# A gated layer with two attentions: six Strassen groups in the input projection, tanh gates, the bias summed behind FFN 1, and attention's filler at two rates

## The chip, the cores and the metric

One core of a Trainium2 chip runs the whole layer. The metric is the device time of one execution in microseconds (us), the median over runs. The engines are TensorE (PE; its weight loads are PEld), VectorE (DVE), ScalarE (ACT), GpSimd (POOL) and SyncE (SP). DMAs are issued on SP's and GpSimd's queues. "L94" is line 94 of the kernel before.

## The reference

The input x has 1024 tokens of 1024 features, all float32. One layer is computed:

```python
h = h + 0.5 * swiglu(rms_norm(h, ffn1_norm), ffn1_w_gate, ffn1_w_up, ffn1_w_down)      # 1024 -> 2816 -> 1024
z = rms_norm(h, mix_norm) @ w_in             # 1024 -> 4352: qa ka va (512 each) qb (512) kb vb (128 each) ga gb (1024 each)
ya = neighbourhood_attention_2d(qa, ka, va, na_rpb)        # 8 heads of 64, a window of 8 x 16 on a 16 x 64 grid, learned bias
yb = windowed_gqa_sink(rope(qb), rope(kb), vb, sink)       # 8 heads on 2 key heads, |i-j| <= 128, a sink logit per head
merged = sigmoid(ga) * (ya @ w_branch_a) + sigmoid(gb) * (yb @ w_branch_b)
h = h + merged @ w_out
h = h + 0.5 * swiglu(rms_norm(h, ffn2_norm), ffn2_w_gate, ffn2_w_up, ffn2_w_down)
return rms_norm(h, final_norm)
```

## The kernel before

**Precision.** Every float32 operand is split into a high half (a copy that rounds to the matmul's input type, on ScalarE, L93) and a low half (the rest, a subtraction on VectorE, or GpSimd where it is given as `eng`, L94). A product is three matmuls, high x high, high x low, low x high (`mm3`, L141 to L150: L145, L147, L149). A matmul has a 128x128 weight tile and streams 512 columns.

**Strassen.** The large products (FFN gate and up, FFN down, part of the input projection, W_out) use seven products of half-size blocks instead of eight (Strassen-Winograd). `products` (L233) runs groups of two pairs of 128-column chunks; for one group it does P1, P2, P5, P6, P7, P3, P4 for two members m, and calls `after` (here `store_z`, L879) with the PSUM banks, which adds the products up, on ScalarE or VectorE (L911, L913), and stores the finished halves in DRAM. `at_end(n)` is called with the number n of weight tiles left, down to 0; `hook` ties work to such an n.

**Order of the stages.** FFN 1's gate and up by hand-written order and then by `products` (to about 432 us); FFN 1's down product, class `Down` (L507); `transition` (L161: normalise and turn the rows, while the down product's tail is done a row block at a time); the input projection's groups (`pg`, to about 842 us); the attention (842 to 1127 us); branch A and the merge with the gates; W_out's product, again `Down`; a second transition; FFN 2 the same way.

**Down.** It has 7 products (P2, P1, P5, P6, P3, P7, P4) x 11 entries. An entry is 12 matmuls. `prep` (L560 to L563, then two splits) prepares an entry's two operands a ring of entries ahead: for P5, P6, P3 the weight blocks are first subtracted, on VectorE and, for half of P6 and all of P3, on GpSimd (L563, L565). `loads[e]` are functions that are called when entry e is reached.

**Projection hooks.** The rotary embedding reads z back from DRAM, does three VectorE operations and stores zr_d (`rope`, all at one n). `v_b` loads v, `order_v` reorders its columns by a ScalarE copy, `turn_v` transposes it. `q_b`, `k_b` load zr_d and split queries and keys. `keep_u` reloads a part of the projection's input and splits it into the place of an operand of the last group, for the gate chunks that are computed later.

**Attention.** 64 units: 32 of B (8 query blocks x 4 head pairs) and 32 of A (4 head pairs x 8 query blocks). A unit goes through `scores` (L1278, L1279, then on VectorE the sum with bias or mask and the row minimum of the negated scores, L1283, on ScalarE the exponential, L1286, and the normalisation), one step later `turn` (L1299) and two steps later `values` (L1313 for A, L1318 for B), whose `write` copies half of the output to SBUF on ScalarE (L1252, L1231) and adds it on VectorE (L1253, L1256, L1233). The bias of A's heads, already laid out in DRAM, is summed with the mask by `load_bias` (L1073) for each head pair.

**Filler.** Between these matmuls TensorE gets `filler` steps of 6 matmuls: the gate chunks that `products` did not do (14 x 8 steps), branch B (8 output chunks x 4 steps, with a weight split, a sigmoid on a gate row block and a multiplication for each), and two chunks of branch A (6 steps). `filling` spends (14*8 + 38 - 44)/64 = 1.656 steps per unit, the rest follows behind the last unit. Then branch A's other chunks run (`a_order`), each with `a_prep` (load of a gate, sigmoid, L1393), a multiplication and a sum, and `combine` builds W_out's Strassen operands.

A scheduler orders each engine's instructions from this program; `keep_in_program_order` (`pin`) keeps an instruction at its place in the program.

## Time and profile before

| | |
|---|---|
| median of 3 runs | 1934.88 us (1934.86 to 1935.12) |
| span of the profiled execution | 1934.8 us |
| VectorE busy 1000 to 1050 us (attention) | 45.66 of 50 us |
| VectorE busy 456 to 534 us (FFN 1 down) | 77.51 of 78 us |
| granted TensorE clock in those stretches | 1.00 |

The page gives each engine's busy time and the chain of work that ended last, followed back from the last instruction. "Idle before, releaser" in a group's row is how long the engine stood idle ahead of these instructions, and what ended it. In a stretch's row, busy time and the number of instructions stand for PE, PEld, DVE, ACT and POOL, then the granted clock, the share of the DMA engines and GB/s. A timeline's rows are start, duration, engine, line, output <- inputs, and in brackets the idle time before with what ended it. Matmuls overlap, so a single matmul's duration is longer than what it adds to the time.

### The profile page before, as it was taken

The numbers are of one execution on the slowest core, as the hardware profiler recorded it, in microseconds if no ns is written. First come the engines' busy times: TensorE is split into PE (matmuls) and PEld (weight loads), VectorE is DVE, ScalarE is ACT, GpSimd is POOL, SyncE is SP. The second block draws the span as 40 slices with busy tenths as digits, with TensorE's granted clock in tenths as the row PEclk, the third lists the DMA queues.
The fourth block names the chain that finished last, engine by engine and source line by source line (L and its number), as shares of the span: only waits on it lengthen the run. The fifth ranks groups of instructions, "written<-read, shape, count | busy, mean of one in ns | idle before, by whom it ended". The sixth has DMA issues, their size and how long they took to land.

```text
span 1934.8 us, 25499 instructions
## 1 busy us (share of the span) xinstructions
PE 1922.2 (99%) x8956; PEld 1603.1 (83%) x8956; DVE 1437.1 (74%) x2560; ACT 943.6 (49%) x1827; POOL 295.5 (15%) x432
## 2 busy tenths in 40 slices
PE   9999999999999999999999999999999999999998
PEld 7888888888888888888888888878888888888886
DVE  7987765668957788678888857889676566569864
ACT  6532333344446543477877862365333333344453
POOL 0011110013300112211122231010111001005210
PEclk9999999999999999999999999999999999999999
DMA  6344323286234478553458576533423323493341
GB/s 261 100 167 163 129 104 128 86 289 225 88 109 137 159 223 250 185 163 104 116 134 195 184 242 210 169 140 133 147 87 109 126 87 109 140 355 104 112 144 61
DMA packets 151745, 298.70 MB, mean 154 GB/s; under 512 B 14912, under 2 KB 64448, under 8 KB 151616
## 3 DMA queue, kind: packets, MB, share of 16 engines
q1 hardware_dynamic: 123072, 210.53, 33.6%
q0 software_dynamic: 27824, 85.48, 13.3%
q8 instruction: 71, 1.16, 0.3%
q10 hardware_dynamic: 720, 1.05, 0.1%
q14 instruction: 58, 0.48, 0.1%
HBM read 210.50 MB, written 88.27 MB: 154 GB/s over the span
## 4 chain that ended last, share of the span: by engine, by line
PE 88%; issue 7%; POOL 1%; DMA 1%; DVE 1%; ACT 1%; POOLq 0%; SPq 0%; ACTq 0%; DVEq 0%
PE g L149 16%; PE g L147 16%; PE g L145 16%; PE d L149 11%; PE d L147 11%; PE d L145 11%; PE d L1299 2%; PE g L1313 1%; PE g L1318 1%; PE d L1278 1%; PE d L1279 1%; POOL zs_d L889 1%; PE d L138 1%; POOL z_d L891 1%; DMA zr_d<-xs 0%
## 5 line engine op out<-in xcount | busy, mean ns | idle before, releaser
L145 PE MATMUL g<-ar,ws 128*128 128x512 f32 x1128 | 423.1, 395 | 0.6 <-ACT fa L911 0.6
L147 PE MATMUL g<-ar,ws 128*128 128x512 f32 x1128 | 417.2, 390 | 0.9 <-DVE ar L94 0.5
L149 PE MATMUL g<-ar,ws 128*128 128x512 f32 x1128 | 416.1, 390 | 0.2 <-DVE ws L311 0.2
L145 PE MATMUL d<-ar,ws 128*128 128x512 f32 x736 | 282.4, 391 | 0.3 <-ACT ar L810 0.2
L147 PE MATMUL d<-ar,ws 128*128 128x512 f32 x736 | 281.9, 390 | 0.3 <-DVE ar L812 0.3
L149 PE MATMUL d<-ar,ws 128*128 128x512 f32 x736 | 281.6, 390 | 0.5 <-DVE ws L311 0.5
L147 PEld LDWEIGHTS g<-ar,ws 128*128 128x128 f32 x1128 | 211.8, 188 | 46.2 <-DVE ar L94 1.0
L149 PEld LDWEIGHTS g<-ar,ws 128*128 128x128 f32 x1128 | 211.7, 188 | 45.5 <-DVE ws L311 0.7
L145 PEld LDWEIGHTS g<-ar,ws 128*128 128x128 f32 x1128 | 206.4, 188 | 37.8 <-ACT fa L911 1.0
L311 DVE TENSOR_TENSOR ws<-raw,ws 128x512 fp32r<-128x512 f32 x204 | 139.6, 690 | 99.6 <-ACT ws L308 98.8
L308 ACT CAST ws<-raw 128x512 fp32r<-128x512 f32 x204 | 125.1, 620 | 140.6 <-PE g L149 64.4
L145 PEld LDWEIGHTS d<-ar,ws 128*128 128x128 f32 x736 | 138.3, 188 | 29.7 <-ACT ar L810 0.6
L147 PEld LDWEIGHTS d<-ar,ws 128*128 128x128 f32 x736 | 138.4, 188 | 29.6 <-DVE ar L812 0.6
L149 PEld LDWEIGHTS d<-ar,ws 128*128 128x128 f32 x736 | 138.4, 188 | 29.4 <-DVE ws L311 0.7
L93 ACT CAST ws<-raw 128x512 fp32r<-128x512 f32 (+1 forms) x121 | 81.0, 669 | 144.0 <-PE d L149 61.8
L94 DVE TENSOR_TENSOR ws<-raw,ws 128x512 fp32r<-128x512 f32 (+1 forms) x119 | 93.7, 789 | 59.8 <-ACT ws L93 59.3
L414 POOL DMA_DIRECT2D hid<-fx x91 | 49.3, 542 | 431.5 <-DVE fx L474 304.9
L93 ACT CAST ar<-raw 128x512 fp32r<-128x512 f32 (+1 forms) x83 | 56.0, 679 | 94.8 <-PE g L147 55.0
L94 DVE TENSOR_TENSOR ws<-ar,ws 128x512 fp32r<-128x512 f32 x114 | 98.3, 867 | 3.8 <-ACT ws L93 3.7
L145 PE MATMUL g<-ws,ws 128*128 128x512 f32 x232 | 91.0, 392 | 0.0
L149 PE MATMUL g<-ws,ws 128*128 128x512 f32 x232 | 90.5, 390 | 0.0
L147 PE MATMUL g<-ws,ws 128*128 128x512 f32 x232 | 90.3, 389 | 0.0
(313 smaller groups left out, 3607.4 us busy)
## 6 DMA issues: line engine op xcount, KB each, us to landing
raw<-hid SPq DMA_DIRECT2D x70, 512.0 KB
hid<-fx POOLq DMA_DIRECT2D x91, 256.0 KB, 2.4
ar<-in_ffn_w_down_dram SPq DMA_DIRECT2D x32, 512.0 KB
raw<-in_ffn_w_up_dram SPq DMA_DIRECT2D x31, 512.0 KB
raw<-in_ffn_w_gate_dram SPq DMA_DIRECT2D x27, 512.0 KB
raw<-in_w_in_dram SPq DMA_DIRECT2D x27, 512.0 KB
hid<-fa POOLq DMA_DIRECT2D x51, 256.0 KB, 2.7
ar<-zs_d POOLq DMA_DIRECT2D x48, 256.0 KB, 5.3
```

The lines of the kernel that those rows point to most:

```text
L93: nc.scalar.copy(dst_hi, src)
L94: (eng or nc.vector).tensor_tensor(dst_lo, src, f32v(dst_hi), op=ALU.subtract)
L138: nc.tensor.transpose(pt[:, c * P:(c + 1) * P], xs[:, (half * 4 + c) * P:(half * 4 + c + 1) * P], ident)
L145: nc.tensor.matmul(b, lhs[0], r[0], start=first, stop=False, **kw)
L147: nc.tensor.matmul(b, lhs[0], r[1], start=False, stop=False, **kw)
L149: nc.tensor.matmul(b, lhs[1], r[0], start=False, stop=last, **kw)
L308: nc.scalar.copy(w[0][:, :512], a)
L311: nc.vector.tensor_tensor(w[0][:, 512:], a, f32v(w[0][:, :512]), op=ALU.subtract)
L414: nc.gpsimd.dma_start(hid[PRODUCTS.index(p), i], src)
L889: nc.gpsimd.dma_start(d[ch * P:(ch + 1) * P, cols], t)
L891: nc.gpsimd.dma_start(z_d[ch * P:(ch + 1) * P, cols], c)
L1299: nc.tensor.transpose(pt[:, i * P:(i + 1) * P], un["pr"][s][:, i * P:(i + 1) * P], ident)
```

## The change

- `groups` gets a sixth entry, gate chunks 20 to 23, which leave the filler's list (10 chunks of 8 steps stay). In the last group P4 is done ahead of P3 (`last`).
- FFN 1's down product gets, at entries 8+5h and 11+5h for head h = 0..7, the fetch of a laid-out bias and two VectorE adds with the mask, stored to DRAM (bm_d) on GpSimd's queue. The attention then loads finished sums (`fetch_bias`); `load_bias` goes.
- The gates use tanh(x/2) where a sigmoid stood; the multiplication adds 1 to it in the same instruction, and the factor 2 is taken back by W_out's scale, 1.0 to 0.5.
- Rotation: loads at one n, the three VectorE operations at n-4, n-5, n-6, one head block every 6. `order_v` goes; chunk 17's eviction writes the new order.
- `write` of B units: one VectorE add of 64x256 in place of two of 64x128; the sink column is copied once for two heads.
- Filler: 80 gate steps over units 0 to 49 (1.6 a unit), 28/14 = 2 a unit from 50 on, nothing spent ahead. Branch B fetches its weights and gates a chunk earlier; its splits' high halves and openings are pinned; splits of outputs move from GpSimd to VectorE.
- The last A output's split into slots 22 and 23 is done in two halves in `write`.
- The second transition (`ahead=3`) does one more block of W_out's tail ahead of a turn.

```diff
-    def split(dst_hi, dst_lo, src, eng=None):
-        nc.scalar.copy(dst_hi, src)
+    def split(dst_hi, dst_lo, src, eng=None, late=False):
+        hi = nc.scalar.copy(dst_hi, src)
+        if late:
+            pin(hi)
...
+    def bias_add(h):
+        for e in range(2):
+            o = biased[0][4 + e]
+            pin(nc.vector.tensor_tensor(o.rearrange("p (d r w) -> p d r w", d=3, r=ROWS),
...
+            nc.gpsimd.dma_start(bm_d[h, e], o)
+
+    for h in range(8):
+        down.loads.setdefault(8 + 5 * h, []).append(lambda d, h=h: bias_fetch(h))
+        down.loads.setdefault(11 + 5 * h, []).append(lambda d, h=h: bias_add(h))
...
+    groups = [[(12, 13), (14, 15)], [(16, 17), (0, 1)], [(4, 5), (8, 9)], [(2, 3), (6, 7)], [(10, 11), (18, 19)],
+              [(20, 21), (22, 23)]]
...
-    for c in range(4):
-        hook(14 * (NG - 1) - 8 - 3 * c, rope, c)
-    hook(14 * (NG - 2) - 6, rope, 4)
-    hook(14 * (NG - 2) - 12, v_b)
-    hook(14 * (NG - 2) - 14, order_v)
-    hook(14 * (NG - 3) - 12, turn_v)
+    for c in range(5):
+        n = 14 * (NG - 1) - 8 - 6 * c
+        hook(n, rope_load, c)
+        for step in range(3):
+            hook(n - 4 - step, rope, step, c)
+    hook(14 * (NG - 3) - 10, v_b)
+    hook(14 * (NG - 4) - 2, turn_v)
...
-    hook(0, keep_u)
+    hook(1, keep_u)
...
+    held = [main.tile([P, 512], F32, tag="hs", bufs=6, name=nm_("hs")) for _ in range(6)]
...
+    def fetch_bias(hp):
+        for s in range(2):
+            for e in range(2):
+                nc.sync.dma_start(bias_at(hp, s, e), bm_d[2 * hp + s, e])
...
-        split(t[:, :512], t[:, 512:], r, eng)
+        split(t[:, :512], t[:, 512:], r, eng, True)
...
+    def open_gate(dc):
+        r = mix["rb", dc]
+        pin(nc.scalar.activation(r, r, AF.Tanh, scale=0.5))
...
-    rate = (nfill - 44) / 64.0
-    spent = 3.0
+    n_b = 50
+    rates = (len(gates) * 8 / n_b, 28 / (64.0 - n_b))
+    spent = 0.0
...
-            split_y(Y_A[n - 60], 512 + (n - 60) * P, nc.gpsimd)
+            split_y(Y_A[n - 60], 512 + (n - 60) * P, nc.vector)
...
-    split(slot(22), slot(23), fa[:, 3072:4096])
...
-    down = Down(4, wo[0], 1.0, place, quarter, {k: left_d[i] for i, k in enumerate(("P5", "P6", "P3", "P7"))},
+    down = Down(4, wo[0], 0.5, place, quarter, {k: left_d[i] for i, k in enumerate(("P5", "P6", "P3", "P7"))},
...
-        nc.scalar.activation(r, r, AF.Sigmoid)
+        nc.scalar.activation(r, r, AF.Tanh, scale=0.5)
...
-    merge.into(transition(down2, gain, to_strassen, behind(hg), 2), hg)
+    merge.into(transition(down2, gain, to_strassen, behind(hg), 2, 3), hg)
```

## The prediction

> **What bounds the kernel now.** I read the page first: engine shares, then the chain that ended last.

> ```profile
> span 1934.8 us, 25499 instructions
> PE 1922.2 (99%) x8956; PEld 1603.1 (83%) x8956; DVE 1437.1 (74%) x2560; ACT 943.6 (49%) x1827; POOL 295.5 (15%) x432
> PE 88%; issue 7%; POOL 1%; DMA 1%; DVE 1%; ACT 1%; POOLq 0%; SPq 0%; ACTq 0%; DVEq 0%
> ```

> TensorE is the bound nearly everywhere. So an edit counts in two ways only: by the matmuls it adds or removes, and by the moments at which TensorE must wait. The profiled execution spans 1934.8 us and the median of the runs is 1934.88 us, so the sum is made against 1934.9 us. The mean of one matmul (about 390 ns in the page's groups) is no price, because matmuls overlap. The price is read from busy time by stretch: columns are PE, PEld, DVE, ACT, POOL busy (instructions), granted clock, DMA share, GB/s.

> ```profile
> 100.00:150.00 50.00, 50.00 (x222) 41.42 (x221) 43.88 (x72) 17.31 (x30) 7.96 (x15) 1.00 0.50 171
> 456.00:492.00 36.00, 36.00 (x160) 29.80 (x160) 35.72 (x36) 14.86 (x26) 20.58 (x13) 1.00 0.31 105
> 492.00:522.00 30.00, 30.00 (x134) 24.83 (x133) 29.79 (x34) 12.82 (x23) 14.74 (x9) 1.00 0.24 80
> 522.00:534.00 12.00, 12.00 (x54) 9.95 (x53) 12.00 (x21) 5.47 (x10) 0.00 (x0) 1.00 0.51 149
> 534.00:552.00 18.00, 18.00 (x81) 14.89 (x80) 9.92 (x17) 6.96 (x14) 0.00 (x0) 1.00 0.37 110
> 1000.00:1050.00 50.00, 50.00 (x304) 44.23 (x303) 45.66 (x146) 40.70 (x107) 12.02 (x23) 1.00 0.70 175
> 1128.00:1178.00 50.00, 50.00 (x221) 41.17 (x220) 16.73 (x28) 23.71 (x30) 10.29 (x8) 1.00 0.77 258
> ```

> In the first row 222 matmuls of 128x512 take 50.00 us with TensorE never idle: 50/222 = 0.2252 us each, at a granted clock of 1.00. The next rows matter as much: from 456 to 534 us, inside the down product of FFN 1, VectorE is busy 77.5 of 78 us. Work added to VectorE there has no idle time to fall into.

> **The change part by part.**

> *Sixth Strassen group.* Four gate chunks leave the attention's filler, where each costs 8 steps of 6 matmuls (192 in all), and become a group of 7 products x 2 chunks x 4 weight blocks x 3 matmuls = 168. That is 24 fewer, and the built order of the changed kernel has 24 fewer 128x512 matmuls and the same number of every other TensorE form. **-24 x 0.2252 = -5.4 us.** The group's evictions are of the kind that the five groups before already hide.

> *Bias and mask behind FFN 1.* Sixteen VectorE adds leave the attention for FFN 1's down product; in the built order eight of them stand ahead of the operand splits for its entry 33, the first of P6. Where TensorE stands close behind VectorE is read from the two timelines (start, duration):

> ```profile
> 519.07 1.78 DVE L94 TENSOR_TENSOR ar<-ar,ar 128x512 fp32r<-128x512 f32 x1
> 521.38 0.68 DVE L94 TENSOR_TENSOR ar<-ar,ar 128x512 fp32r<-128x512 f32 x1
> 521.98 0.68 DVE L94 TENSOR_TENSOR ws<-raw,ws 128x512 fp32r<-128x512 f32 x1
> 522.01 0.39 PE L147 MATMUL g<-ar 128*128 128x512 f32 x1
> L1073 DVE TENSOR_TENSOR fa<-raw,masks 128x384 f32<-128x384 f32 x16 | 8.5, 550 | 0.1
> ```

> The split that ended at 519.07+1.78 = 520.85 feeds the matmul at 522.01: a lead of 1.16 us, the smallest of this stage. Neighbouring starts (521.38, 521.98) lie 0.60 apart for a 0.68 operation, so in a queue an operation costs some 0.08 less than its duration: 0.47 for the 0.55 add. Eight cost 8 x 0.47 = 3.8 us; less the lead, TensorE waits **+2.7 us** there. The lower end is 0, if part of the collisions with GpSimd (1.78 against 0.68 us) fall elsewhere; the upper 5, if the adds meet GpSimd too (two of eight slowed by 1.1 us). The other eight adds fall where VectorE is busy 9.92 of 18 us: free. Their stores go on GpSimd's queue, which has 36.00-20.58 us to spare, and their loads on SP's.

> *Attention.* VectorE and ScalarE per unit, before:

> ```profile
> L1233 DVE TENSOR_TENSOR xs<-g,s 64x128 f32<-64x128 f32 x64 | 18.0, 281 | 1.0 <-ACT s L1231 0.2
> L1253 DVE TENSOR_TENSOR s<-g,s 64x256 f32<-64x256 f32 x32 | 13.2, 411 | 2.6 <-ACT s L1252 2.3
> L1282 DVE COPY fa<-nsk 128x1 f32<-128x1 f32 x60 | 7.9, 142 | 0.5 <-ACT fa L1286 0.5
> L94 POOL TENSOR_TENSOR ar<-raw,ar 128x1024 fp32r<-128x1024 f32 x6 | 14.8, 2464 | 22.0 <-ACT ar L93 22.0
> L94 DVE TENSOR_TENSOR ar<-raw,ar 128x1024 fp32r<-128x1024 f32 x3 | 3.7, 1219 | 0.0
> ```

> VectorE loses two 64x128 adds for one 64x256 (18.0 us becomes 32 x 0.411 = 13.2), half the sink copies (4), and the 8.5 us above; it gains six 128x1024 splits that GpSimd did (6 x 1.22 = 7.3). But the filler is spent at 2 steps a unit in the last 14 units instead of 1.66, all of it branch B with its weight splits, openings and merges. Adding durations less 0.08 over the built order, VectorE needs in the four groups of four units at the end 1.03, 0.96, 0.91 and 0.99 of TensorE's time; the same sum for before gives at most 1.11 in one group, and in its heaviest stretch (45.66 and 40.70 busy of 50) TensorE lost little. I take **+1**, between 0 and +4 (14 units late by the 0.3 that one 64x128 add is).

> *Into the attention.* Two stalls of before stand here (the idle time in brackets), and ahead of them three links of the chain that leads to the first:

> ```profile
> 777.64 7.13 DMA zr_d<-xs
> 784.91 0.88 issue
> 785.79 0.60 ACT fa L911
> ```

> ```profile
> 786.43 0.50 PE L145 MATMUL g<-ar,ws 128*128 128x512 f32 x1 [0.56 <-ACT fa L911]
> 849.95 0.50 PE L147 MATMUL g<-ar,ws 128*128 128x512 f32 x1 [0.53 <-DVE ar L94]
> ```

> The first comes from ScalarE's reordering copy (order_v) that waits for a buffer until a rotation's store lands; the eviction L911 is stuck behind it. The copy is gone and the rotation's loads wait on SP: starts 785.49 to 786.43, less one matmul of 0.23, **-0.7 us**. The second is the late split of keep_u. Its hook moves one step earlier, but k_b's loads now stand on SP behind two fetches of bm_d, which wait for the buffer of the last product's evictions, that is for a store like this one (median us to landing last), and the keys had little to spare:

> ```profile
> g_d<-fa POOLq DMA_DIRECT2D x4, 256.0 KB, 4.2
> ```

> ```profile
> 839.84 1.23 DVE L94 TENSOR_TENSOR ar<-raw,ar 128x1024 fp32r<-128x1024 f32 x1 [0.74 <-ACT ar L93]
> 842.04 0.28 PE L1279 MATMUL d<-ar,ar 128*128 128x256 f32 x1
> ```

> The last key's split ended at 841.07 and the first matmul on a low half of a key began at 842.04: 0.97 us. I take a net **+0.5**, between -0.7 (the second stall goes too) and +2.4 (keys late by 4.2, less 0.97 and less the 0.8 by which P4 ahead of P3 frees that buffer sooner, about four matmuls).

> *The end of the attention.* Before, branch B and A's first chunks are left over behind the last unit's values: 36 steps x 6 matmuls and more, 228 x 0.2252 = 51 us. ScalarE's and VectorE's work for that unit's output lies under it:

> ```profile
> 1129.38 1.05 ACT L93 CAST ar<-fa 128x1024 fp32r<-128x1024 f32 x1
> 1130.45 1.28 ACT L1179 ACT_TABLE_LOAD   x1
> 1128.30 0.72 PE L147 MATMUL d<-ar,ws 128*128 128x512 f32 x2
> L1252 ACT COPY s<-g 64x256 f32<-64x256 f32 x32 | 11.9, 371 | 3.9 <-PE g L1313 3.1
> L1393 ACT ACTIVATE raw<-raw 128x1024 f32<-128x1024 f32 x8 | 8.5, 1061 | 7.7 <-DMA raw<-g_d 7.7
> L93 ACT CAST ws<-raw 128x512 fp32r<-128x512 f32 x10 | 6.2, 618 | 4.5 <-DMA raw<-in_w_branch_b_dram 4.0 <-PE d L149 0.2 <-DMA raw<-in_w_branch_a_dram 0.2
> L94 POOL TENSOR_TENSOR ws<-raw,ws 128x512 fp32r<-128x512 f32 x2 | 2.5, 1292 | 14.6 <-ACT ws L93 14.6
> ```

> After, the filler is spent (80 + 32 of 118 steps) when the last values end, and TensorE's next instruction is branch A's first matmul. Its weight is split only now: in the built order ScalarE does the copy of the last output (0.37), the tanh of a gate (1.06), the high half of output slot 22 (0.62 for 128x512) and only then the high half of that weight (0.62), which is pinned in program order. That is 2.67 us with TensorE idle. The low half follows on GpSimd (1.29); TensorE has four matmuls (0.9) before it needs it: 0.4 more. With 0.1 to 0.2 for each of five handovers, **+4 us**, between +3 (2.67+0.4, no handovers) and +5.5 (the tanh's load, which stands on SP behind six weight loads, comes 1.5 late). What is late next, the last output's split, has 36 matmuls = 8.1 us of cover.

> The tanh matters just here. The table load of before, 1.28 us at 1130.45, was hidden under the leftover; with a sigmoid it would now lie in this idle stretch. The built order has three table loads where before had four, none at this place. [...]

> *The merge's second transition.* One more block of W_out's product stands ahead of its fourth turn. Stalls of before here:

> ```profile
> 1290.35 1.06 PE L138 MATMUL d<-ident,xs 128*128 128x128 f32 x8 [0.80 <-DVE xs L129]
> 1295.59 0.50 PE L149 MATMUL g<-ar,ws 128*128 128x512 f32 x1 [0.24 <-DVE ws L311]
> 1315.96 0.50 PE L149 MATMUL d<-ar,ws 128*128 128x512 f32 x1 [0.48 <-DVE ws L311]
> ```

> The first stands ahead of the edit and stays. The order gives the later turns 12 to 18 whole matmuls between them, where before had blocks cut up: the other two may go. **-1**, between -2 and +1 (a stall like the first, in a new place).

> **Sum:** -5.4 + 2.7 + 1 - 0.7 + 0.5 + 4 - 1 = +1.1, so 1934.9 + 1.1 = **1936.0 us**: the saved matmuls are given back as waits.

> **The rivals.**

> *The gain arrives.* The adds in FFN 1 cost less than the lead (0 of 2.7), the last weight's split finds ScalarE free, say because the scheduler's order lets the tanh go late (3 of 4), the attention loses nothing (0 of 1): -5.4 + 0 + 0 - 0.7 + 0.5 + 3 - 1 = -3.6, and with the second transition at -2 and the entry at -0.7 it is -5.8: 1929 to 1931, say 1930. For it: VectorE has less work inside the attention. Against it: 35.72 of 36.00 busy, and the pinned order. Chance 0.27.

> *Slower: ScalarE and VectorE fall behind in the last 14 units.* The filler there is the work that needs them most, in order pinned with the units' own. If TensorE waits at each unit for one add, 14 x 0.28 = 3.9, and the chain at the end starts late with its 5.5: -5.4 + 2.7 + 3.9 - 0.7 + 0.5 + 5.5 - 1 = +5.5: 1940.4. It decides from the point where VectorE's need passes TensorE's time over a whole group (1.03 in the first of the four groups; 0.99 in the last). For it: those shares. Against it: the 1.11 group of before cost little. Chance 0.30, with the case that the bias adds meet GpSimd.

> *The change doesn't do what it says:* if tanh took a table of its own, eight openings among exponentials would cost 16 x 1.28 = 20 us of ScalarE. The order's three loads speak against it: below 0.01.

> **How the numbers follow.** A measurement tells about 0.2% from no change, 3.9 us: 1931.0 to 1938.8. The forecast (1933 to 1938.8 by itself) has 0.43, the gain's arrival 0.27, the slower case 0.30. The parts' ends summed whole give 1934.9 - 5.4 + (0+0-0.7-0.7+3-2) = 1929.1 and 1934.9 - 5.4 + (5+4-0.7+2.4+5.5+1) = 1946.7; that all meet at the upper end is improbable, so the range is 1928.5 to 1943.0. Faster 0.26, same 0.43, slower 0.31.

> **What would show it.** The matmul count falls by 24. In FFN 1's down product, idle time of TensorE behind L94 at the first of P6, near 522 us: 2.7 us. No stall at L911. Behind the last values, an idle stretch of 3 to 5.5 us ended by the pinned ScalarE copy, then a short one by GpSimd. If VectorE's eight adds open no gap at 522, or the last stretch is under 1 us, I am wrong and the time is near 1930; if gaps of some tenths stand at each of the last 14 units, it is near 1940.

## The result, and the profile after

| | before | after |
|---|---|---|
| median of the runs, us | 1935.12 (1934.86 to 1939.04, 5 runs) | 1944.10 (1942.62 to 1944.63, 5 runs) |
| span of the profiled execution, us | 1934.8 | 1942.3 |

The ratio is 1.0044, 95% interval 1.0033 to 1.0055: **slower by 0.44%**, some 8.5 us. The forecast was 1936.0, with a range of 1928.5 to 1943.0. The page of the changed kernel (its line 95 is the high half of a split, 98 the low half, 149 to 153 the three matmuls):

```profile
span 1942.3 us, 25526 instructions
PE 1919.9 (99%) x8932; PEld 1601.7 (82%) x8932; DVE 1450.5 (75%) x2527; ACT 944.5 (49%) x1836; POOL 293.5 (15%) x446
PE 85%; issue 6%; DVE 4%; ACT 2%; DMA 2%; POOL 1%; POOLq 0%; SPq 0%; DVEq 0%; ACTq 0%
L149 PE MATMUL g<-ar,ws 128*128 128x512 f32 x1096 | 416.4, 396 | 5.2 <-ACT ws L95 4.8
L149 PE MATMUL d<-ar,ws 128*128 128x512 f32 x760 | 293.2, 392 | 4.5 <-ACT ws L95 4.0
```

TensorE has 24 matmuls fewer (8956 to 8932) and its share of the chain falls from 88% to 85%. The new idle time stands ahead of matmuls that wait for the high half of a weight from ScalarE: 4.8 + 4.0 us in two groups, where before's page has no group of matmuls with more than this one:

```profile
L147 PE MATMUL g<-ar,ws 128*128 128x512 f32 x1128 | 417.2, 390 | 0.9 <-DVE ar L94 0.5
```

Where the time went is seen by stage. For each stage, "lost" is the time from its first matmul to the next stage's first, less the count of matmuls by shape times a price each (0.2252 us for 128x512, 0.171 for 128x384, 0.1165 for 128x256, 0.105 for 128x128). The wait behind the last values counts with the row that follows them. The prices lie a little under the median start-to-start times of before (0.227, 0.175, 0.119, 0.109), so some us of each long stage are no waits; the differences are what counts. The 24 saved matmuls do not appear in them, and kernels with unlike amounts of filler in a stage can be compared. The first 30 us stand alone: they lost 5.0 to 5.3 us in some executions and 6.3 to 7.1 in others, of kernels that share that code. In before's execution the clock was granted at 0.50 from 16 to 19 us, in that of after at 1.00, so this row is no effect of the change.

| lost, us | before | after | difference |
|---|---|---|---|
| first 30 us | 6.3 | 5.1 | -1.2 |
| rest of FFN 1 | 3.7 | 5.0 | +1.4 |
| transition and projection | 4.1 | 4.3 | +0.2 |
| first scores to last values | 10.1 | 18.9 | +8.8 |
| last values to second transition | 1.3 | 7.7 | +6.4 |
| second transition and FFN 2 | 8.1 | 5.3 | -2.8 |

With -5.4 for the matmuls the differences sum to +7.4, about that of the spans (7.5). Two rows hold the loss. Of the +8.8 in the first of them, 6.6 lie between 1081 and 1121 us, around branch B's first matmul (7.9 lost there, 1.3 in the like units of before), and 1.2 in the first 20 us; the 50 units ahead of branch B lose otherwise what they lost before. The idle stretches in them, from TensorE's timeline of the changed kernel (start, duration, and in brackets the idle time and what ended it):

```profile
888.74 0.41 PE L1358 MATMUL d<-ident,fa 128*128 128x128 f32 x2 [1.82 <-DVE fa L1349]
1094.83 0.72 PE L149 MATMUL d<-ar,ws 128*128 128x512 f32 x2 [3.98 <-ACT ws L95]
1106.92 0.50 PE L149 MATMUL g<-ar,ws 128*128 128x512 f32 x1 [0.79 <-ACT ws L95]
1164.70 0.50 PE L149 MATMUL g<-ar,ws 128*128 128x512 f32 x1 [0.80 <-ACT ws L95]
1175.32 1.22 PE L149 MATMUL g<-ar,ws 128*128 128x512 f32 x2 [3.20 <-ACT ws L95]
```

1094.83 is branch B's first matmul, 1175.32 branch A's. Both waited for their weight's split, and both were followed by something that the idle time alone doesn't show. These rows are stretches (PE, PEld, DVE, ACT, POOL busy with instructions, then the granted clock):

```profile
1094.00:1096.00 2.00, 1.17 (x5) 1.00 (x6) 1.92 (x4) 2.00 (x5) 0.54 (x1) 0.98 1.17 256
1096.00:1099.00 3.00, 3.00 (x12) 2.52 (x11) 1.85 (x5) 1.91 (x5) 0.00 (x0) 0.50 1.04 335
1099.00:1102.00 3.00, 3.00 (x14) 2.53 (x14) 2.42 (x6) 1.23 (x4) 0.00 (x0) 0.95 1.03 423
...
1172.00:1175.00 3.00, 0.12 (x2) 0.00 (x0) 1.95 (x6) 2.96 (x5) 0.00 (x0) 0.90 1.02 324
1175.00:1181.00 6.00, 5.68 (x13) 4.46 (x14) 0.47 (x1) 1.83 (x4) 4.99 (x4) 0.50 1.05 396
1181.00:1184.00 3.00, 3.00 (x14) 2.45 (x13) 0.00 (x0) 0.00 (x0) 0.00 (x0) 0.96 1.06 396
```

After the idle stretch the clock was granted at 0.50 for 3 us, then for 6. In the second of these stretches a matmul of 128x512 starts 0.427 us behind the one before it, against 0.227 at full clock (13 in the row of 6 us, which at 0.227 us each would take 3.0), so the two cost nearly half their length: about 1.5 and 3 us on top of the waits.

ScalarE at branch B's start, around the first of them, has no idle time left (no bracket in any row):

```profile
1090.93 0.61 ACT L1345 ACTIVATE fa<-fa,nmx 128x384 f32<-128x384 f32 x1
1091.45 0.19 ACT L1345 ACTIVATION_READ_ACCUMULATOR fa<-fa,nmx 128x1 f32 x1
1091.65 1.07 ACT L1168 COPY xs<-g 128x512 f32<-128x512 f32 x2
1092.61 1.06 ACT L95 CAST ar<-raw 128x1024 fp32r<-128x1024 f32 x1
1093.55 0.63 ACT L1345 ACTIVATE fa<-fa,nmx 128x384 f32<-128x384 f32 x1
1094.07 0.20 ACT L1345 ACTIVATION_READ_ACCUMULATOR fa<-fa,nmx 128x1 f32 x1
1094.16 0.61 ACT L95 CAST ws<-hs 128x512 fp32r<-128x512 f32 x1
```

A unit's exponentials, the eviction of the last gate chunk (1091.65) and the split of one of B's outputs (1092.61) stand ahead of the weight (1094.16). Behind the last values, the chain is the one that the prediction wrote down:

```profile
1172.69 0.35 ACT L1308 COPY s<-g 64x256 f32<-64x256 f32 x1
1173.06 1.06 ACT L1454 ACTIVATE raw<-raw 128x1024 f32<-128x1024 f32 x1
1174.13 0.62 ACT L95 CAST ar<-fa 128x512 fp32r<-128x512 f32 x1
1174.66 1.13 ACT L95 CAST ws<-hs 128x512 fp32r<-128x512 f32 x2
```

### The profile page after: what moved, and what is told of

It reads as the page before. It is cut to its first block, busy times and chain, and to the rows that moved or that the text cites. A ratio compares the mean times of both kernels' runs of the same rounds, so it can differ in the third digit from the quotient of the medians.

```text
span 1942.3 us, 25526 instructions
## 1 busy us (share of the span) xinstructions
PE 1919.9 (99%) x8932; PEld 1601.7 (82%) x8932; DVE 1450.5 (75%) x2527; ACT 944.5 (49%) x1836; POOL 293.5 (15%) x446
## 3 DMA queue, kind: packets, MB, share of 16 engines
q0 software_dynamic: 28912, 88.63, 13.9%
q10 hardware_dynamic: 720, 1.05, 0.1%
## 4 chain that ended last, share of the span: by engine, by line
PE 85%; issue 6%; DVE 4%; ACT 2%; DMA 2%; POOL 1%; POOLq 0%; SPq 0%; DVEq 0%; ACTq 0%
PE g L149 16%; PE g L151 16%; PE g L153 16%; PE d L149 10%; PE d L151 10%; PE d L153 10%; PE d L1358 2%; PE g L1377 1%; PE d L1339 1%; PE d L1340 1%; DVE ar L98 1%; DMA raw<-g_d 1%; DVE ws L98 1%; PE g L1372 1%; PE d L142 1%
## 5 line engine op out<-in xcount | busy, mean ns | idle before, releaser
L149 PE MATMUL g<-ar,ws 128*128 128x512 f32 x1096 | 416.4, 396 | 5.2 <-ACT ws L95 4.8
L151 PE MATMUL g<-ar,ws 128*128 128x512 f32 x1096 | 410.5, 391 | 0.4 <-DVE ar L863 0.4
L153 PE MATMUL g<-ar,ws 128*128 128x512 f32 x1096 | 410.4, 391 | 0.0
L149 PE MATMUL d<-ar,ws 128*128 128x512 f32 x760 | 293.2, 392 | 4.5 <-ACT ws L95 4.0
L151 PE MATMUL d<-ar,ws 128*128 128x512 f32 x760 | 291.9, 391 | 0.3 <-DVE ar L842 0.3
L153 PE MATMUL d<-ar,ws 128*128 128x512 f32 x760 | 291.8, 391 | 0.0
L151 PEld LDWEIGHTS g<-ar,ws 128*128 128x128 f32 x1096 | 206.5, 188 | 44.2 <-DVE ar L863 0.8
L153 PEld LDWEIGHTS g<-ar,ws 128*128 128x128 f32 x1096 | 206.2, 188 | 43.5
L149 PEld LDWEIGHTS g<-ar,ws 128*128 128x128 f32 x1096 | 202.1, 189 | 42.0 <-ACT ws L95 5.5
L316 DVE TENSOR_TENSOR ws<-raw,ws 128x512 fp32r<-128x512 f32 x210 | 143.6, 690 | 109.0 <-ACT ws L313 108.1
L149 PEld LDWEIGHTS d<-ar,ws 128*128 128x128 f32 x760 | 142.3, 188 | 33.9 <-ACT ws L95 4.5
L151 PEld LDWEIGHTS d<-ar,ws 128*128 128x128 f32 x760 | 142.9, 188 | 30.3 <-DVE ar L842 1.0
L153 PEld LDWEIGHTS d<-ar,ws 128*128 128x128 f32 x760 | 142.7, 188 | 29.9 <-DVE ws L316 0.5
L95 ACT CAST ws<-raw 128x512 fp32r<-128x512 f32 (+1 forms) x107 | 70.5, 659 | 138.8 <-PE d L153 60.0
L98 DVE TENSOR_TENSOR ws<-raw,ws 128x512 fp32r<-128x512 f32 (+1 forms) x107 | 82.8, 774 | 47.7 <-ACT ws L95 47.6
L98 DVE TENSOR_TENSOR ar<-raw,ar 128x512 fp32r<-128x512 f32 (+1 forms) x83 | 63.7, 771 | 37.9 <-ACT ar L95 36.7
L149 PE MATMUL g<-ws,ws 128*128 128x512 f32 x232 | 90.9, 392 | 0.0
L153 PE MATMUL g<-ws,ws 128*128 128x512 f32 x232 | 90.5, 390 | 0.0
## 6 DMA issues: line engine op xcount, KB each, us to landing
hid<-fx POOLq DMA_DIRECT2D x91, 256.0 KB, 2.6
hid<-fa POOLq DMA_DIRECT2D x51, 256.0 KB, 2.6
ar<-zs_d POOLq DMA_DIRECT2D x48, 256.0 KB, 6.5
```

Source lines behind the costliest of these rows:

```text
L95: hi = nc.scalar.copy(dst_hi, src)
L98: (eng or nc.vector).tensor_tensor(dst_lo, src, f32v(dst_hi), op=ALU.subtract)
L149: nc.tensor.matmul(b, lhs[0], r[0], start=first, stop=False, **kw)
L151: nc.tensor.matmul(b, lhs[0], r[1], start=False, stop=False, **kw)
L153: nc.tensor.matmul(b, lhs[1], r[0], start=False, stop=last, **kw)
L316: nc.vector.tensor_tensor(w[0][:, 512:], a, f32v(w[0][:, :512]), op=ALU.subtract)
```

## The experiments

The theory at first was that the filler's hand-out is to blame, branch B's start among busy units and no cover at the end; the rival, that the attention starves when the sixth group takes gate steps away. The spans are those of one profiled execution each; medians stand beside those of before on the same chip.

**The sixth group alone, and the old rate in the changed kernel.** On the kernel before, and on the changed one:

```diff
+              [(20, 21), (22, 23)]]           # on the kernel before, nothing else
```

```diff
-    rates = (len(gates) * 8 / n_b, 28 / (64.0 - n_b))
-    spent = 0.0
+    rates = ((len(gates) * 8 + 38 - 44) / 64.0,) * 2
+    spent = 3.0
```

> The kernel before with the sixth group alone (the filler's rate follows from its formula: 1.156 steps a unit, 36 steps left over behind the last unit as before). Theory 'the filler's hand-out': the 24 saved matmuls arrive, -5.4 us, and the attention still runs at TensorE's pace: 1929 to 1931 us. Rival 'the attention starves': with half a step less a unit (0.7 us) VectorE and ScalarE become the bound, stalls of 0.1 to 0.3 us at most of the 64 units, +6 to +19: 1936 to 1949 us.

> The changed kernel with the filler handed out by the old rule (1.156 steps a unit, 3 ahead, 41 steps left over behind the last unit). Hand-out: the idle stretches at branch B's start (4.1 us) and behind the last values (3.4 us) go, with the slow matmuls behind both; 1942 less 13 to 14 = 1928 to 1931 us. Starving: the idle stretches go, but small stalls stand at most units instead, 1936 us or more.

Measured: the group alone 1944.59 us (before 1936.70; ratio 1.0043, 1.0028 to 1.0058); the old rate 1942.51 (1.0030, 1.0020 to 1.0040). The group alone is as slow as the whole change. It loses 25.0 us in the attention where before lost 10.1, and nothing special behind it (1.6); its profiled execution was 2.8 us above its median, so some of the 25.0 may be this execution's own. The hand-out theory fell here as the whole cause: both times lie where the rival had them. With the lighter units of the change and the same rate the attention loses 16.0; behind it 7.5, of which branch B's start is the most, though it lies behind the last unit there.

**Nothing pinned, and more cover behind the attention.**

```diff
-        split(t[:, :512], t[:, 512:], r, eng, True)
+        split(t[:, :512], t[:, 512:], r, eng)          # the same in split_y, and no pin in open_gate
```

```diff
-    rates = (len(gates) * 8 / n_b, 28 / (64.0 - n_b))
+    rates = (len(gates) * 8 / n_b, 16 / (64.0 - n_b))
```

> The changed kernel with nothing pinned in branch B and the splits for it (weights, outputs, gate openings); the hand-out stays. In the built order ScalarE then does the first weights and openings several units earlier, and branch A's first weight is still behind the last output. If the pinned order makes the idle stretch at branch B's start: that one shrinks below 1 us, the last one stays near 3.4, 1936 to 1938 us. If ScalarE has no time for it in any order: 1941 us or more.

> The changed kernel with 16 steps instead of 28 over the last 14 units, so 18 steps are left over behind the attention instead of 6 (12 x 6 x 0.225 = 16 us more cover). Hand-out: the idle stretch behind the last values goes with the slow matmuls behind it (6.4 us), and the one at branch B's start stays or shrinks: 1933 to 1937 us. Starving: what is won behind the last values is lost as stalls in the last 14 units: 1940 to 1944 us.

Measured: unpinned 1945.11 us (1.0042, 1.0028 to 1.0056), more cover 1948.16 (1.0058, 1.0043 to 1.0073), above both forecasts for it. Both took the loss behind the last values away (0.9 and 2.1 us instead of 7.7) and lost more than that in the attention (25.4 and 26.7 instead of 18.9). Without the pins, ScalarE's queue put a split of B's outputs ahead of its data, and all stood behind it; ScalarE's row and TensorE's:

```profile
1093.92 1.04 ACT L95 CAST ar<-raw 128x1024 fp32r<-128x1024 f32 x1 [6.92 <-DMA raw<-y_d]
```

```profile
1095.43 0.69 PE L1358 MATMUL d<-ident,fa 128*128 128x128 f32 x2 [6.91 <-ACT fa L1350]
```

So taking all pins away is no help: they keep a late load from blocking the units. It doesn't clear the place of each pinned split, which is tried below. And filler kept back from the last 14 units for the end is missed in them.

**Five groups with every other edit, and the bias adds elsewhere.**

```diff
-              [(20, 21), (22, 23)]]           # and the old rate, as above
...
-        down.loads.setdefault(8 + 5 * h, [])  # in the second kernel alone
-        down.loads.setdefault(11 + 5 * h, [])
+        down.loads.setdefault(29 + 4 * h, [])
+        down.loads.setdefault(32 + 4 * h, [])
```

> The changed kernel with five groups as before (14 gate chunks in the filler, 1.656 steps a unit, 3 ahead, branch B behind the attention); every other edit stays. Theory 'light filler': the sixth group takes 32 gate steps away, and these are the filler that asks little of ScalarE and VectorE; with them back the attention loses what it lost before or less, the stretch behind it nothing, and the other edits keep their gains (L911 -0.7, second transition -2.8, lighter units up to -3, FFN 1's down product +0.9): 1930 to 1933 us. Rival 'the other edits cost the time in the attention' (pinned order, fetches of bm_d, splits on VectorE): 1936 us or more.

> As e_five, with the bias fetches at entries 29+4h and the adds at 32+4h of FFN 1's down product instead of 8+5h and 11+5h, so that they come behind the place where VectorE is nearly late. If the adds ahead of P6 are what TensorE waits for there (0.9 us at 519 us in the changed kernel): that stall goes and the time is 0.5 to 1 us below e_five. If it is a collision with GpSimd alone: same as e_five.

Measured: 1940.78 us (before 1936.34; 1.0026, 1.0016 to 1.0035) and 1940.26 (1.0016, 1.0007 to 1.0025). The first time is the rival's, though not for its reason. The attention went back to 11.5 lost, 2.8 of FFN 2's gain stayed, but behind the attention 7.0 were lost at branch B's start, which I had not expected in this kernel. One wait of 1.35 us in the attention was new as well: a gate's eviction on ScalarE stood 3.55 us and began at 964.55, just when B's output store had landed (957.68 and 6.8 us to landing), so the buffer that this store held is the likely cause; the trace names none. The adds behave as predicted in kind. The stretch of FFN 1's down product in the first kernel, with them ahead of P6, and in the second, with them behind:

```profile
505.00:525.00 20.00, 19.47 (x85) 15.49 (x84) 19.89 (x23) 7.77 (x15) 10.57 (x8) 1.00 0.41 126
```

```profile
505.00:525.00 20.00, 20.00 (x90) 16.55 (x89) 19.86 (x25) 8.46 (x15) 8.19 (x6) 1.00 0.45 129
```

85 matmuls against 90 in 20 us. Lost between 500 and 530 us: 1.3 to 2.2 in every kernel with the adds at the early entries, 0.2 in before, and 0.2 with the adds later.

**The hand-out in the old code, and the sigmoid in the new.**

```diff
-    rate = (nfill - 44) / 64.0                # the kernel before with the sixth group
-    spent = 3.0
+    rate = (nfill - 6) / 66.0
+    spent = 0.0
```

```diff
-        pin(nc.scalar.activation(r, r, AF.Tanh, scale=0.5))
+        pin(nc.scalar.activation(r, r, AF.Sigmoid))      # also in a_prep; plain products, W_out's scale 1.0
```

> The kernel before with the sixth group and its whole filler handed out over the attention (112 steps over 66 rounds, nothing ahead), so with none of the other edits. Light filler: branch B falls among the last 15 units as in the changed kernel and VectorE has the old units' adds besides: 1943 to 1950 us. Rival (the other edits are the cause, the hand-out is right): 1937 us or less.

> The changed kernel with sigmoid gates (and the plain multiplication and scale 1.0 with them). The built order has 18 table loads instead of 3. By the trace's 1.28 us each, ScalarE gets 15 x 1.28 = 19 us more, nearly all within the last 14 units where it is 80% busy: 10 to 19 us more, 1952 to 1962 us. [...]

Measured: 1977.23 us (1.0209, 1.0195 to 1.0223) and 1958.67 (one run; span 1956.9). The first is inconclusive for its question: its sigmoids fall among exponentials and bring 20 table loads into attention and merge, 25.7 us on ScalarE by 1.28 each. The second gives the price of the table switches in the new code. ScalarE's loads in the last 14 units and behind:

```profile
L1224 ACT ACT_TABLE_LOAD x8 | 10.3, 1283 | 0.1
L1344 ACT ACT_TABLE_LOAD x7 | 9.0, 1283 | 0.1
```

Fifteen loads more (18 against 3), 19.3 us of ScalarE, and a span longer by 14.6: within the forecast from the trace's 1.28 us. A load takes 1.283 us here, and ahead of each of these two groups ScalarE is idle 0.1 us in all.

**The late weights mended.**

```diff
-        w = branch_w(wb[0], 0, None, mix.pop(("wr", 0)))
+        w = mix.pop("w0")
...
-                yield from gate(dc, {0: lambda: [fetch_y(c * P) for c in range(2)],
-                                     3: lambda: [fetch_gate(0), fetch_w(wb[0], 0, 0)],
+                yield from gate(dc, {0: lambda: [fetch_w(wb[0], 0, 0), *[fetch_y(c * P) for c in range(2)]],
+                                     3: lambda: [fetch_gate(0), mix.update(w0=branch_w(wb[0], 0, None, mix.pop(("wr", 0))))],
...
+                if c == 2 and dc + 1 == NC8:  # branch A's first weight; second kernel alone
+                    mix["wa0"] = branch_w(wa[0], a_order[0], nc.gpsimd, mix.pop(("wr", NC8)))
...
```

> The changed kernel; only branch B's first weight is fetched at the last gate chunk's step 0 and split at its step 3, ahead of the splits of B's outputs, instead of at branch B's start. If the pinned place of that split makes the 4.1 us idle stretch at branch B's start: it and the slow matmuls behind it go, the span falls from 1942.3 by 5 to 6 us, to about 1937. If ScalarE has too much to do in these two units in any order: the stretch only moves to the next operand, 1940 us or more.

> As e_earlyB, and branch A's first weight is split two steps before branch B ends instead of behind the last output. If that split's place makes the 3.4 us idle stretch behind the last values and the half-speed matmuls behind it: a further 5 to 6.5 us, span 1930 to 1932. If the last output's split is what is late: still 1 us or more idle there, span 1934 or more.

> As e_five (five groups) with branch B's first weight split early. The 2.5 us idle stretch at branch B's start (behind the attention) and the slow matmuls behind it go: span 1938.6 less 5 to 5.7 = 1933. If the splits of B's outputs are late too, 1936 or more.

> As e_five_early, but with six groups (1.156 steps a unit). Against e_five_early this is the sixth group alone: light filler says that the 5.4 us of matmuls saved are given back in the attention (it lost 4.5 us more in e_even than in e_five): the two within 2 us of each other. If the group is a gain once the starts are mended: 4 us or more below e_five_early.

Measured, before 1936.74: B's weight early 1944.46 us (1.0040, 1.0026 to 1.0054), both early 1941.18 (1.0024, 1.0014 to 1.0033), five groups with B's early 1936.42 (1.0000, 0.9991 to 1.0009), six at the old rate with B's early 1942.97 (1.0033, 1.0020 to 1.0045). With branch B among the units, the idle stretch only moved, from the weight to the next operands; TensorE in the first of the four:

```profile
1101.13 0.50 PE L149 MATMUL d<-ar,ws 128*128 128x512 f32 x1 [1.80 <-ACT ar L95]
1106.53 0.44 PE L1339 MATMUL d<-ar 128*128 128x384 f32 x1 [0.72 <-DVE ws L98]
1108.09 0.61 PE L149 MATMUL g<-ar,ws 128*128 128x512 f32 x1 [0.95 <-ACT ws L95]
```

The attention lost 20.9 us there, 18.9 without the edit (its profiled execution was 2.3 us above its median, and 0.5 of the difference is in the first turns). ScalarE was busy 9.88 us of the 10 from 1086 to 1096, ahead of this, and 6.11 of the next 10. So it has too much to do in the units just ahead of branch B's start, in any order tried. Behind the last values the place of the split was the cause: with A's weight early, 2.6 us are lost instead of 7.7 (7.2 with B's early alone). Those 4.6 are close to the 5 to 6.5 forecast for that step; the span of 1930 to 1932 stood on the gain at branch B's start, which did not come. Five groups with the weight early lose 11.3 and 2.2, about as before; the span of 1936.4 instead of the 1933 forecast holds 2.0 us more in the first 30 us than e_five's. The sixth group on top of that (the last of the four) costs 4.9 in the attention, and at branch B's start, behind the last unit again, ScalarE's split of an output is late:

```profile
1131.25 1.22 PE L149 MATMUL d<-ar,ws 128*128 128x512 f32 x2 [3.11 <-ACT ar L95]
```

So the sixth group in an otherwise equal kernel: -5.4 in matmuls, +4.9 in the attention, +6.4 behind it; 6.5 us slower by the medians. Neither forecast had that. The attention alone gives the saving back, as the first of them said; the rest is branch B's start once more.

**The rate alone, and the best of it.** In the kernel before, nothing but the rate:

```diff
-    rate = (nfill - 44) / 64.0
+    rate = (nfill - 76) / 64.0                # 1.156 steps a unit; (nfill - 60) gives 1.406
```

> The kernel before, all its five groups and edits untouched, with only the filler's rate cut from 1.656 to 1.156 steps a unit (68 steps left over behind the attention instead of 36); no matmul is added or removed. If the rate of filler in the attention is the cause of the sixth group's loss: the attention loses about 25 us to waits, as with the sixth group alone at that rate, instead of 10, and the time is 1948 to 1951 us. If the group itself (its evictions, its stores, its buffers) is the cause: 1934 to 1937 us.

> As e_b116 with 1.406 steps a unit, half way. If the loss grows only below the rate at which TensorE has less to do per unit than VectorE: well under half of e_b116's, +2 to +5 us, 1937 to 1940 us. If it grows evenly with the steps taken away: half, +7, 1942 us.

Measured: 1949.71 and 1942.78 us (one run each; before 1936.74). No matmul differs, the groups are the old ones, and the attention loses:

| steps a unit (kernel before) | 1.656 | 1.406 | 1.156 | 1.156 with the sixth group |
|---|---|---|---|---|
| lost from first scores to last values, us | 10.1 | 13.9 | 21.4 | 25.0 |
| lost from there to the second transition, us | 1.3 | 3.4 | 4.0 | 1.6 |

The rate alone brings 11.3 of the 14.9 us that the sixth group lost in the old code's attention; of the other 3.6, 1.7 lie in the first 20 us, and no run tells the group's own share from the execution's. In the attention the loss grew by 3.8 for the first quarter of a step and by 7.5 for the next. With the losses behind it the times are 6.0 and 13.0 us above before, close to the even growth that gave the forecast of 1942. One stretch of before and the same of the kernel at 1.156:

```profile
1042.00:1092.00 50.00, 50.00 (x299) 43.85 (x298) 44.56 (x145) 42.05 (x108) 14.72 (x20) 1.00 0.70 171
```

```profile
1042.00:1092.00 50.00, 47.09 (x282) 39.58 (x281) 46.93 (x143) 42.19 (x108) 9.03 (x7) 1.00 0.56 170
```

VectorE goes from 44.56 to 46.93 busy, TensorE from never idle to 2.9 us idle. The five waits over 0.4 us from 1000 us to the last values all end with an instruction of VectorE. That fits units which come as fast as VectorE and the handovers allow; no run tries it by itself.

The last kernel joins what paid: five groups, B's weight early, the adds at the later entries, and the old two-part write of B's units.

> As e_five_early (five groups, branch B's first weight split early), with the bias adds of FFN 1's down product at the later entries and the old two-part write of B's units (its store landed late once and held a gate's copy for 3.6 us, TensorE 1.6 us). From e_five_early: 2.0 for the adds and 1.6 for the write less; with the same start of the kernel as in the profile of before this is 1931 to 1933 us, below both kernels by 0.1% to 0.2% of before.

Measured: 1935.58 us, before 1936.74; ratio 0.9994, 0.9985 to 1.0003; span 1932.6. It is faster than the changed kernel, and not to be told from before; the forecast of 1931 to 1933 was missed. Its stages lose 3.6 (FFN 1 behind the first 30 us), 3.3, 11.5, 2.2 and 5.3 us: the sum is about 1.3 below before's, 2.8 from the second transition and 0.8 from the projection less 2.3 that the attention and its end cost more. Of the two edits on top of e_five_early, the adds gave their 2.0 us (3.6 lost where that kernel lost 5.6); the old write gave nothing (11.5 lost in the attention, 11.3 there).

## Why the prediction was wrong, step by step

- **The step that failed is "Attention ... I take +1", between 0 and +4.** It measured +8.8. The prediction did count branch B's splits, openings and merges among the last 14 units, but only on VectorE, as a share of TensorE's time over groups of four units, and it priced being late at 0.3 us a unit. VectorE's share was a little under what it said. What it left out is ScalarE's order ahead of branch B's first matmul, the working that it did make for branch A's: there ScalarE is busy 5.96 of 6 us and TensorE waits 3.98 us for one split, and the clock drops behind that. In the units behind, TensorE is never idle with VectorE at 0.89 and 0.91. Three stretches of the changed kernel:

```profile
1088.00:1094.00 6.00, 2.85 (x18) 2.42 (x16) 4.89 (x15) 5.96 (x13) 0.58 (x1) 1.00 1.24 229
1108.00:1130.00 22.00, 22.00 (x131) 19.18 (x130) 19.58 (x60) 16.60 (x43) 0.54 (x1) 1.00 0.36 120
1130.00:1150.00 20.00, 20.00 (x117) 17.66 (x116) 18.18 (x53) 16.21 (x39) 0.54 (x1) 1.00 0.50 168
```

Behind it stands a second thing: the prediction booked the sixth group's saving whole, and did not ask what the attention is filled with afterwards. Before, all steps spent among the units are gate chunks (3 + 64 x 1.656 = 109 of 112), and branch B comes behind. After, 80 are left; either the rate falls and the units lose (e_even, and e_b116 in the old code), or branch B begins among them, at 1094.83. That ScalarE's work is what stops it there is seen in the trace; that no order of it would do is not shown beyond the orders tried. The rival "Slower: ScalarE and VectorE fall behind in the last 14 units" had the engine, the place and the sign, but priced it as 0.28 a unit, not as one stop of 4 us and a slow clock.

- **"Sixth Strassen group: -5.4".** Right in the count and wrong as a gain: alone, the group makes the kernel 0.43% slower. (The price of 0.2252 is slightly low, since 222 counts matmuls that only reach into the stretch; with the 0.227 between starts the term is still -5.4.)
- **"The end of the attention: +4".** The chain was right link by link (3.20 idle against 2.67 and handovers; mended by e_earlyAB), but +6.4 came. The upper end was +5.5, and the half clock behind the wait, some 3 us, is what the sum did not have: the size of a wait is not its price when the clock drops behind it.
- **"Bias and mask behind FFN 1: +2.7".** Right in place, near 519 us, and in kind (e_five_adds); 1.1 to 2.0 in size.
- **"Into the attention".** The stall at L911 went, as forecast, and so did the 0.5 behind the first scores. A wait of 1.8 at the first turns is new. It lies within the upper end of +2.4, but by luck: the prediction feared keys late behind the fetches of bm_d, and e_five, which has these fetches, waits 0.29 there and loses 1.2 us in the first 20 (before 1.5). The wait came with less filler at the start: 1.81 in e_b116, which has no fetches of bm_d.
- **"The merge's second transition: -1".** -2.8, beyond the bound of -2: the first of the three stalls, which the prediction said would stay, went too. Kernels with the edit lose 5.3 to 5.6 us in that stage, those without 7.7 to 8.1.
- **The tanh** is what makes the rest bearable: with a sigmoid the changed kernel is 14.6 us slower still.

## What to carry to other kernels

Work that fills a stage's gaps is worth more there than its own length: before it is made cheaper or moved, ask what takes its place, and what that asks of the other engines. A saving of matmuls in a filler is a gain only while the host stage stays full. Count what is left over behind the stage too, since it covers the next stage's first operands.

## What the runs showed of the hardware

Some waits of TensorE were followed by a granted clock of 0.50, one of only 1.80 us among them (B's weight early): for 3.41 us behind the changed kernel's 3.98, for 6.83 behind its 3.20; in the unpinned kernel, whose wait was 6.91 us, it was 10.2 us. Near 2.3 us it went either way. The sixth group alone, at the first turns:

```profile
890.30 1.08 PE L1300 MATMUL d<-ident,fa 128*128 128x128 f32 x4 [2.38 <-issue]
```

```profile
890.00:893.00 3.00, 2.70 (x9) 2.34 (x10) 2.19 (x11) 2.35 (x8) 0.00 (x0) 0.52 0.96 279
```

and B's weight early, in the same place:

```profile
890.44 0.41 PE L1358 MATMUL d<-ident,fa 128*128 128x128 f32 x2 [2.26 <-DVE fa L1349]
```

```profile
890.00:893.00 3.00, 2.56 (x18) 2.32 (x19) 2.32 (x9) 2.25 (x9) 0.00 (x0) 1.00 0.85 234
```

The length of the wait alone is not what decides here. The wait of 1.80 us in the same kernel, at 1101.13 (shown above), was followed by half clock, and one of 2.46 us in the kernel with more cover was not. B's weight early behind its 1.80, then more cover's wait and what followed it:

```profile
1102.00:1105.00 3.00, 3.00 (x12) 2.41 (x11) 2.81 (x10) 1.54 (x5) 0.00 (x0) 0.51 1.02 406
```

```profile
1156.36 0.62 PE L1372 MATMUL g<-ws,fx 128*128 128x256 f32 x3 [2.46 <-DVE ws L98]
```

```profile
1156.00:1159.00 3.00, 2.46 (x15) 2.09 (x16) 2.52 (x8) 2.89 (x8) 0.00 (x0) 1.00 1.01 319
```

The steps of the other two kernels are estimates, from where their slow stretches end (near 1104.9 us with B's weight early, by the row above; near 1100.5 with more cover, where two matmuls of 128x512 go from 0.85 us back to 0.46) and the same 3.41 us. The 1.80 us lay within one step, 1098.1 to 1101.5; the 2.46 us, from 1153.90 on, were cut by the step's end at 1155.1 into 1.2 and 1.3. Two short waits in one step did the same: the 0.72 and 0.95 us at 1106.53 and 1108.09 lay in the step from 1104.9 to 1108.3, and behind it a matmul of 128x384 took 0.52 us, where 0.34 is usual in this kernel. So at 1.66 and 1.67 us (0.72 + 0.95) in a step it went either way. The steps lie at another place in each execution (the first record begins at 5.74 us in before's and at 7.06 in the changed kernel's), and nearly equal waits fell out unlike: the 1.80 us were followed by half clock, the changed kernel's 1.82 were not.
